# First block of a hybrid encoder step: g read from PSUM, other banks for the fourth tile, pinned casts and products, one weight's upper parts cast by GpSimd

## The chip, the core and the metric

The kernel runs on one core of one Trainium2 chip. A core has five engines that run their own instruction queues and meet at semaphores: TensorE (PE, whose weight loads are listed apart as PEld), VectorE (DVE), ScalarE (ACT), GpSimd (POOL) and SyncE (SP, which here only issues transfers). The metric is the device time of one launch in microseconds (us); lower is better. The median of three runs is given.

## The reference

One layer over 2048 prompt frames and 32 sample frames of width 1024 (2080 rows in all):

```python
def layer(h, p, ...):
    hn = rmsnorm(h, g_mix)
    proj = hn @ w_in                       # 1024 x 3072
    hA, bA, cA, zA, vB, zB = split(proj)   # six pieces of width 512
    yA = bA * conv3(cA * hA) * silu(zA)
    yB = pooled(vB) @ pool_w * pool_scale * silu(zB)
    h = h + concat(yA, yB) @ w_out
    gate = sigmoid(rmsnorm(h, g_ple) @ w_ple_gate)
    return h + (p @ w_ple) * gate
```

A last RMSNorm closes it; the last rows of `cA * hA` and `vB` are returned as states. `rmsnorm` multiplies each row by one over the root of its mean square, and each column by g. The change touches the first product alone: `hn @ w_in` for the first frames.

## The kernel before

**Precision.** Every float32 operand of a product is split in two fp32r parts (`split`, L77): `hi` is a cast, `lo` is the operand minus `hi`. A product is three: hi x hi, hi x lo, lo x hi. The cast runs on ACT (L78), the difference on DVE (L79).

**Blocks.** The rows are cut into five blocks of 416 frames (`NB`). Blocks 0 and 1 are the first group. A block comes in as four tiles of x: three of 128 rows and a short one of 32; the short tile of block 0 (`short0`, 64 rows) holds the 32 rows of block 0 and those of block 1 together. Each tile is loaded by SP (L393), its squares are summed on ACT (L89), POOL makes the root in two steps (`ms`, L70, and `rstd`, L74), DVE scales the tile by the root and by g (`normal`, L407), PE turns it in two halves of four 128-column pieces each (`turn`, L417), and the turned halves are split into the operand `B0` (`put`): "11" and "21" for block 0, "12" and "22" for block 1. From the parts of both blocks DVE makes differences (f, L659) for later products.

**g.** g_mix comes in as one row; PE spreads it over 128 partitions with a matrix of ones, in two halves of 512 columns, each into a bank of PSUM (`gm_0`, `gm_1`, L376). DVE copies both into `g_bc` in SBUF (L377), and all scaling reads `g_bc`.

**PSUM.** There are eight banks: six in the ring of `bank` and two in the ring of `tbank`. In block 0 the turned halves (`pt0_...`) take the six large ones, the fourth tile's two halves come round to the first ones again. `idle` is a small bank into which PE turns the identity, to no purpose but to be busy (`keep_busy`, L618; 30 times in all).

**The first products.** Three weights of unit 0 come first: zb, v and c (`weights`, their raw forms are `raw_first...`, whose space first serves as scrap for the squares). For each, the hi x hi part of block 0 is made first (`upper_parts`, L582, tiles `zb_first`, `v_first`, `c_first`), the parts with lo follow (`lower_parts`), then block 1 by `project` (L565, tiles `zb`, `v`, `c`). In between PE turns block 1's tiles (`pt1_...`) and the small vectors (`pv`, L694). Block 1's short part is turned first (`pt1_3_...`), since it lies in the tile that is there already; ACT also copies each turned half of block 1 back over its tile (L657), which frees the bank.

**Order.** A scheduler orders the instructions of each engine; those marked by `keep_in_program_order` stay in the order of the program. Every engine runs its queue strictly in order, so an instruction that waits holds all behind it.

Of the kernel before, what the change touches and what calls it, by code (L numbers as in the profile page):

```python
# [12 lines left out]
ALU = mybir.AluOpType  # L13
PSUM = bass.MemoryType.PSUM

P = 128
D = 1024
# [18 lines left out]
def trunk(ctx, tc, x_p, x_s, c_conv, c_pool, p_p, p_s, g_mix, w_in, conv_w, conv_b, pool_w,  # L36
# [39 lines left out]

    def split(hi, lo, src, eng=nc.vector):  # L77
        ins = nc.scalar.copy(hi, src)  # L78
        eng.tensor_tensor(lo, src, hi.bitcast(F32), op=ALU.subtract)  # L79
        return ins  # L80
# [250 lines left out]
    with ExitStack() as s1:  # L331
# [16 lines left out]

        def put(piece, src):

            return split(piece[:, :, 0], piece[:, :, 1], src)

# [18 lines left out]
        ones = ftile("ones").rearrange("p k n -> p (k n)")[:1, :P]  # L371
        nc.vector.memset(ones, 1.0)
        for half in range(2):
            cs = slice(half * NH, half * NH + NH)
            pg = tbank(f"gm_{half}")
            nc.tensor.matmul(pg, ones, gm_row[:, cs], start=True, stop=True)  # L376
            nc.vector.tensor_copy(g_bc[:, cs], pg)  # L377


# [24 lines left out]

        def normal(x, later=False, cs=slice(0, D)):
            xt, n, r = x
            ins = nc.vector.scalar_tensor_tensor(xt[:n, cs], xt[:n, cs], r[:n], g_bc[:n, cs], op0=ALU.mult,  # L407
                                                 op1=ALU.mult)
            if later:
                tc.keep_in_program_order(ins)  # L410

        def turn(x, half, name, get=tbank, later=False):
            xt, n, _ = x
            pt = get(name)
            for k in range(KH):
                kk = half * KH + k
                ins = nc.tensor.transpose(pt[:, k * P:k * P + n], xt[:n, kk * P:(kk + 1) * P], ident[:n, :n])  # L417
# [101 lines left out]

        def weights(kind, j, name):  # L520

            if first_w:
                return first_w.pop(0)
            raw = raw_weight(kind, j, name, lambda name: raw_of.pop(kind) if kind in raw_of else raw_ring(name))
            out = []
            for half in range(2):
                out.append(wtile(f"w_{name}_{half}"))
                put(out[-1], raw[:, half * KH:half * KH + KH])
            return out
# [30 lines left out]

        def half_product(ps, lhs, b, start, stop=True):

            for k in range(KH):
                for q, (x, y) in enumerate(((0, 0), (0, 1), (1, 0))):
                    nc.tensor.matmul(ps[:, :NB], lhs[:, k, x], b[:, k, y], start=start and k + q == 0,  # L565
                                     stop=stop and k == KH - 1 and q == 2, skip_group_check=True)

        begun = {}

        def project(ps, w, tb, between=None):  # L570
            x = hn[tb]
            for half in range(2):
                half_product(ps, w[half], x[half], half == 0, half == 1)
                if between and not half:
                    between()
# [9 lines left out]
        def upper_parts(kind, w, tb):  # L585

            ps = bank(f"{kind}_first")
            for half in range(2):
                part_of(ps, w, tb, half, 0, 0, start=half == 0)
            begun[kind] = ps  # L590
# [21 lines left out]
        B0.update(six(0))  # L612
        idle = tbank("idle")

        def keep_busy(n):

            for _ in range(n):
                tc.keep_in_program_order(nc.tensor.transpose(idle[:, :P], ident, ident))  # L618
# [21 lines left out]
        def second_block():  # L640
# [8 lines left out]
            for c, cs in [spans[3], *spans[:3]]:  # L649
# [60 lines left out]
        class Unit:  # L710
# [44 lines left out]
            def mix(self, b):  # L755
# [955 lines left out]
```

## Time and profile before

| | us |
|---|---|
| median of three runs (920.5 to 921.92) | 921.82 |
| the profiled execution, whole | 921.55 |
| its span, first to last instruction | 919.8 |
| PE busy in the span | 907.4 (99%) |
| DVE busy | 723.6 (79%) |
| ACT busy | 478.9 (52%) |
| POOL busy | 153.6 (17%) |

The granted TensorE clock is 0.998 of full speed over the span. Times in a trace are counted from the span's start; a row of a timeline gives start, duration, engine, line, operation, what it writes and reads, how many are merged, and in brackets the idle time before it with what ended it. A row of the chain of waits gives start, length and the work that everything later waited for. A busy time of merged rows runs from the first start to the last end; on DVE and ACT one instruction starts some 0.08 before the one ahead has ended.

### The profile page before, as it was taken

The numbers are of one execution on the slowest core, as the hardware profiler recorded it, in microseconds if no ns is written. First come the engines' busy times: TensorE is split into PE (matmuls) and PEld (weight loads), VectorE is DVE, ScalarE is ACT, GpSimd is POOL, SyncE is SP. The second block draws the span as 40 slices with busy tenths as digits, with TensorE's granted clock in tenths as the row PEclk, the third lists the DMA queues.
The fourth block names the chain that finished last, engine by engine and source line by source line (L and its number), as shares of the span: only waits on it lengthen the run. The fifth ranks groups of instructions, "written<-read, shape, count | busy, mean of one in ns | idle before, by whom it ended". The sixth has DMA issues, their size and how long they took to land.

```text
span 919.8 us, 13006 instructions
## 1 busy us (share of the span) xinstructions
PE 907.4 (99%) x4515; PEld 821.9 (89%) x4515; DVE 723.6 (79%) x1235; ACT 478.9 (52%) x883; POOL 153.6 (17%) x271
## 2 busy tenths in 40 slices
PE   8999999999999999999999999999999999999996
PEld 7999999999999999999999987888877868878885
DVE  6996989999488989785778679665554798888875
ACT  7744565554345555443545446344334875465555
POOL 4111322212001111000000011111111002323333
PEclk9999999999999999999999999999999999999999
DMA  8255595769935555457765359756775885799892
GB/s 261 79 156 151 162 274 157 210 201 314 414 114 162 181 160 187 118 178 264 203 177 170 125 192 295 254 190 184 252 216 170 307 263 146 185 222 241 205 264 101
DMA packets 140734, 186.37 MB, mean 203 GB/s; under 512 B 12060, under 2 KB 111260, under 8 KB 139389
## 3 DMA queue, kind: packets, MB, share of 16 engines
q1 hardware_dynamic: 120237, 126.33, 45.1%
q0 software_dynamic: 17696, 53.71, 20.0%
q10 hardware_dynamic: 2736, 5.51, 1.8%
q8 instruction: 35, 0.57, 0.3%
q14 instruction: 30, 0.25, 0.1%
HBM read 128.93 MB, written 56.56 MB: 202 GB/s over the span
## 4 chain that ended last, share of the span: by engine, by line
PE 89%; DVE 4%; DMA 3%; ACT 1%; issue 1%; SPq 0%; POOL 0%; DVEq 0%; ACTq 0%; POOLq 0%
PE x_o L168 9%; PE x_zbv L565 7%; PE x_ch L565 7%; PE x_zab L565 7%; PE x_g L168 6%; PE e L103 5%; PE z_o L168 4%; PE z_zbv L565 3%; PE z_ch L565 3%; PE z_zab L565 3%; PE b L565 3%; PE za L565 3%; PE h L565 3%; PE z_g L168 3%; PE v L565 2%; PE c L565 2%
## 5 line engine op out<-in xcount | busy, mean ns | idle before, releaser
L103 PE MATMUL e<-wq,pps 128*128 128x512 f32 (+1 forms) x156 | 38.9, 399 | 0.2 <-ACT pps L78 0.2
L78 ACT CAST y_S<-y_fS 128x512 fp32r<-128x512 f32 x32 | 19.3, 621 | 38.0 <-PE x_o L168 20.0
L168 PE MATMUL x_o<-wo_b,y_S 128*128 128x512 f32 x128 | 35.7, 390 | 0.0
L168 PE MATMUL x_g<-wg_b,g_S 128*128 128x512 f32 x128 | 35.7, 389 | 0.0
L565 PE MATMUL z_zbv<-B,w_zbv_S 128*128 128x416 f32 x168 | 34.2, 352 | 0.0
L565 PE MATMUL x_ch<-B,w_ch_S 128*128 128x416 f32 x168 | 34.1, 351 | 0.0
L565 PE MATMUL z_zab<-B,w_zab_S 128*128 128x416 f32 x168 | 34.1, 351 | 0.0
L565 PE MATMUL x_zab<-B,w_zab_S 128*128 128x416 f32 x168 | 34.0, 351 | 0.0
L565 PE MATMUL x_zbv<-B,w_zbv_S 128*128 128x416 f32 x168 | 34.0, 351 | 0.0
L565 PE MATMUL z_ch<-B,w_ch_S 128*128 128x416 f32 x168 | 34.0, 351 | 0.0
L1438 POOL DMA_DIRECT2D e<-h_d x28 | 24.9, 908 | 53.8 <-DVE e L1435 46.3
L103 PEld LDWEIGHTS e<-wq,pps 128*128 128x128 f32 (+1 forms) x156 | 27.4, 182 | 6.9 <-ACT pps L78 0.5
L70 POOL TENSOR_SCALAR ms_x<-ssq_x 128x1 f32<-128x1 f32 (+2 forms) x18 | 12.3, 682 | 122.7 <-ACT junk L89 118.5
L565 PEld LDWEIGHTS x_zab<-B,w_zab_S 128*128 128x128 f32 x168 | 31.3, 188 | 0.4
L565 PEld LDWEIGHTS x_zbv<-B,w_zbv_S 128*128 128x128 f32 x168 | 31.4, 188 | 0.3
L565 PEld LDWEIGHTS z_ch<-B,w_ch_S 128*128 128x128 f32 x168 | 31.4, 188 | 0.3
L565 PEld LDWEIGHTS z_zab<-B,w_zab_S 128*128 128x128 f32 x168 | 31.3, 188 | 0.3
L565 PEld LDWEIGHTS x_ch<-B,w_ch_S 128*128 128x128 f32 x168 | 31.3, 188 | 0.3
L565 PEld LDWEIGHTS z_zbv<-B,w_zbv_S 128*128 128x128 f32 x168 | 31.3, 188 | 0.4
L78 ACT CAST y<-y 128x512 fp32r<-128x512 f32 x24 | 14.8, 618 | 30.8 <-PE z_o L168 12.8
L168 PEld LDWEIGHTS x_o<-wo_b,y_S 128*128 128x128 f32 x128 | 24.0, 188 | 5.1 <-ACT c_o L1241 0.3
L168 PEld LDWEIGHTS x_g<-wg_b,g_S 128*128 128x128 f32 x128 | 24.0, 188 | 4.9
(607 smaller groups left out, 2656.2 us busy)
## 6 DMA issues: line engine op xcount, KB each, us to landing
y<-y_d SPq DMA_DIRECT2D x16, 512.0 KB, 6.2
x<-in_x_prompt_dram SPq DMA_DIRECT2D x16, 512.0 KB, 5.7
h_d<-x SPq DMA_DIRECT2D x16, 512.0 KB, 2.6
hn<-h_d SPq DMA_DIRECT2D x61, 128.0 KB, 6.6
xt<-in_x_prompt_dram SPq DMA_DIRECT2D x15, 512.0 KB, 5.3
e<-e_d SPq DMA_DIRECT2D x15, 512.0 KB, 6.1
e<-h_d POOLq DMA_DIRECT2D x28, 256.0 KB, 7.0
out_dram<-e POOLq DMA_DIRECT2D x13, 512.0 KB, 4.1
```

Of the source, the lines that this page charges most:

```text
L70: nc.gpsimd.tensor_scalar(ms[:n], ssq[:n], scalar1=1.0 / D, scalar2=EPS, op0=ALU.mult, op1=ALU.add)
L78: ins = nc.scalar.copy(hi, src)
L103: nc.tensor.matmul(ps[:n], pps[:, a, k, :n], wp[k][b][:, cs], start=k + q == 0, stop=k == 1 and q == 2)
L168: nc.tensor.matmul(ps[:n], lhs[:, k, a, :n], w[b][:, k], start=start and k + q == 0, stop=k == KH - 1 and q == 2, skip_group_check=True)
L565: nc.tensor.matmul(ps[:, :NB], lhs[:, k, x], b[:, k, y], start=start and k + q == 0, stop=stop and k == KH - 1 and q == 2, skip_group_chec ...
L1438: nc.gpsimd.dma_start(ee, h_d[r:r + P, at[1] * NH:at[1] * NH + NH], accum_op=ALU.add)
```

## The change

It has six parts, all in the first block:

1. **Scaling.** Block 0's four tiles are scaled by halves (`normal_half`) that read g from its two PSUM banks. The copies into `g_bc` stay, ahead of the scaling in DVE's queue; block 1's tiles and all later scaling read `g_bc` as before.
2. **Banks.** The short tile's halves are turned into the two small banks (those of g), for block 0 and for block 1.
3. **Fillers.** `idle` goes. Fillers (17 instead of 30) are written into the bank that the next transposes or `zb_first` will overwrite.
4. **Pins.** The casts of v's and c's first weights, the products of block 1 (`project` with `tb == 1`) and the first product of `mix` stay in program order.
5. **zb's casts.** The hi parts of zb's first weight are cast by POOL (`nc.gpsimd.tensor_copy`), two casts of 128x512.
6. `split`, `put` and `weights` take the casting operation as an argument.

```diff
-    def split(hi, lo, src, eng=nc.vector):
-        ins = nc.scalar.copy(hi, src)
+    def split(hi, lo, src, eng=nc.vector, cast=nc.scalar.copy):
+        ins = cast(hi, src)
         eng.tensor_tensor(lo, src, hi.bitcast(F32), op=ALU.subtract)
         return ins
...
+        g_ps = []
         for half in range(2):
...
             nc.vector.tensor_copy(g_bc[:, cs], pg)
+            g_ps.append(pg)
...
+        def normal_half(x, half):
+            xt, n, r = x
+            cs = slice(half * NH, half * NH + NH)
+            tc.keep_in_program_order(
+                nc.vector.scalar_tensor_tensor(xt[:n, cs], xt[:n, cs], r[:n], g_ps[half][:n], op0=ALU.mult, op1=ALU.mult))
+
+        def turn(x, half, name, get=tbank, later=False, fill=0):
             xt, n, _ = x
             pt = get(name)
+            for _ in range(fill):
+                tc.keep_in_program_order(nc.tensor.transpose(pt[:, :P], ident, ident))
...
-        def weights(kind, j, name):
+        def weights(kind, j, name, cast=nc.scalar.copy):
...
-                put(out[-1], raw[:, half * KH:half * KH + KH])
+                ins = put(out[-1], raw[:, half * KH:half * KH + KH], cast)
+                if name[:5] == "first" and kind != "zb":
+                    tc.keep_in_program_order(ins)
...
-                half_product(ps, w[half], x[half], half == 0, half == 1)
+                half_product(ps, w[half], x[half], half == 0, half == 1, tb == 1)
...
             ps = bank(f"{kind}_first")
+            for _ in range(4 if kind == "zb" else 0):
+                tc.keep_in_program_order(nc.tensor.transpose(ps[:, :P], ident, ident))
...
-        keep_busy(8)
+        FILL = (6, 1), (1, 1), (4, 1), (0, 0)
         for x in (*ahead0, short0):
             for half in range(2):
-                normal(x, True, slice(half * NH, half * NH + NH))
+                normal_half(x, half)
...
-                ins = put(B0[q][:, :, :, c * P:c * P + n], turn(x, half, f"pt0_{c}_{half}", bank, True)[:, :, :n])
+                ins = put(B0[q][:, :, :, c * P:c * P + n], turn(x, half, f"pt0_{c}_{half}", bank if c < 3 else tbank, True, FILL[c][half])[:, :, :n])
                 tc.keep_in_program_order(ins)
-                keep_busy(((1, 1), (1, 12), (1, 1), (3, 2))[c][half])
...
-            made.append(weights(kind, 0, f"first{kind}"))
+            made.append(weights(kind, 0, f"first{kind}", nc.gpsimd.tensor_copy if kind == "zb" else nc.scalar.copy))
...
-                    pt = turn(x, half, f"pt1_{c}_{half}", bank, later=True)[:, :, ts]
+                    pt = turn(x, half, f"pt1_{c}_{half}", tbank if c == 3 else bank, later=True)[:, :, ts]
...
-                nc.tensor.matmul(pm[:, :NB], pw[:, 0, j], pp, start=True, stop=False)
+                ins = nc.tensor.matmul(pm[:, :NB], pw[:, 0, j], pp, start=True, stop=False)
+                if self.gi + j == 0:
+                    tc.keep_in_program_order(ins)
```

The order of the instructions changes on PE, DVE and ACT in the first 75 us, and hardly behind. PE, from the second tile's second half to the first product (a transpose reads `ident`; rows with `ident` alone are fillers; `pt0_2` is the third tile, `pt0_3` the short one). Before:

```order
L417 MATMUL pt0_1_1_239<-ident_70,xt_0_1_170 128x128 x4
L618 MATMUL idle_198<-ident_70 128x128 x12
L417 MATMUL pt0_2_0_258<-ident_70,xt_0_2_178 128x128 x4
L618 MATMUL idle_198<-ident_70 128x128
L417 MATMUL pt0_2_1_266<-ident_70,xt_0_2_178 128x128 x4
L417 MATMUL pt0_3_0_274<-ident_70,xt_0_3_186 128x64 x4
L618 MATMUL idle_198<-ident_70 128x128 x3
L417 MATMUL pt0_3_1_284<-ident_70,xt_0_3_186 128x64 x4
L618 MATMUL idle_198<-ident_70 128x128 x2
L582 MATMUL zb_first_360<-B0_0_195,w_firstzb_0_294 128x416 x4
```

Now:

```order
L426 MATMUL pt0_1_1_235<-ident_70,xt_0_1_170 128x128 x4
L423 MATMUL pt0_2_0_243<-ident_70 128x128 x4
L426 MATMUL pt0_2_0_243<-ident_70,xt_0_2_178 128x128 x4
L423 MATMUL pt0_2_1_254<-ident_70 128x128
L426 MATMUL pt0_2_1_254<-ident_70,xt_0_2_178 128x128 x4
L426 MATMUL pt0_3_0_262<-ident_70,xt_0_3_186 128x64 x4
L426 MATMUL pt0_3_1_269<-ident_70,xt_0_3_186 128x64 x4
L602 MATMUL zb_first_343<-ident_70 128x128 x4
L595 MATMUL zb_first_343<-B0_0_195,w_firstzb_0_277 128x416 x4
```

Four fillers stand ahead of the third tile where twelve did, none between the short tile's halves, and four ahead of the first product. On ACT the two casts of zb, which stood ahead of and behind the short tile's second cast, are gone; on POOL they stand behind the short tile's root and ahead of block 1's first root.

DVE, from block 1's last scaling (`xt_1_2`) to the low part of its first turned half (`pt1_3_0`); w_h is the next weight, V the values of block 0. Before:

```order
L407 SCALAR_TENSOR_TENSOR xt_1_2_318<-xt_1_2_318,rstd_x1_2_337,g_bc_84 128x1024
L79 TENSOR_TENSOR pw_343<-raw_pw_352,pw_343 128x512
L79 TENSOR_TENSOR w_h0_0_0_656<-raw_h0_0_654,w_h0_0_0_656 128x4x128
L782 TENSOR_TENSOR win1_0_0_0_0_422<-V_0_0_356 128x416
L79 TENSOR_TENSOR B0_12_320<-pt1_3_0_430,B0_12_320 128x4x32
```

Now:

```order
L409 SCALAR_TENSOR_TENSOR xt_1_2_301<-xt_1_2_301,rstd_x1_2_320,g_bc_84 128x1024
L79 TENSOR_TENSOR pw_326<-raw_pw_335,pw_326 128x512
L791 TENSOR_TENSOR win1_0_0_0_0_409<-V_0_0_339 128x416
L79 TENSOR_TENSOR B0_12_303<-pt1_3_0_417,B0_12_303 128x4x32
L800 TENSOR_TENSOR pl_0_0_0_0_411<-win1_0_0_0_0_409,cnt_110 128x1
```

The difference of w_h has moved behind (it follows block 1's low parts now).

DVE, from the pooled values' low part (pp) to the low parts of block 1's third tile (`pt1_2`), the last that block 1's products need. Before:

```order
L79 TENSOR_TENSOR pp_0_0_421<-pl_0_0_0_0_424,pp_0_0_421 128x416
L79 TENSOR_TENSOR B0_2_197<-pt1_0_1_454,B0_2_197 128x4x128
L79 TENSOR_TENSOR B0_12_320<-pt1_1_0_462,B0_12_320 128x4x128
L79 TENSOR_TENSOR B0_2_197<-pt1_1_1_470,B0_2_197 128x4x128
L695 COPY vec_342<-pv_478 128x112
L79 TENSOR_TENSOR B0_12_320<-pt1_2_0_491,B0_12_320 128x4x128
L659 TENSOR_TENSOR f0_1_0_580<-xt_1_0_307,B0_0_195 128x512
L79 TENSOR_TENSOR B0_2_197<-pt1_2_1_499,B0_2_197 128x4x128
```

Now:

```order
L79 TENSOR_TENSOR pp_0_0_408<-pl_0_0_0_0_411,pp_0_0_408 128x416
L702 COPY vec_325<-pv_465 128x112
L79 TENSOR_TENSOR B0_12_303<-pt1_1_0_449,B0_12_303 128x4x128
L666 TENSOR_TENSOR f0_1_0_567<-xt_1_0_290,B0_0_195 128x512
L79 TENSOR_TENSOR B0_2_197<-pt1_1_1_457,B0_2_197 128x4x128
L79 TENSOR_TENSOR B0_12_303<-pt1_2_0_478,B0_12_303 128x4x128
L79 TENSOR_TENSOR B0_2_197<-pt1_2_1_486,B0_2_197 128x4x128
```

One difference (f0) has moved ahead of the low part of `pt1_2_0`, and the low part of `pt1_0_1` ahead of pp.

More of the change, by code (lines that the diff above doesn't have):

```diff
@@ L347, in wtile, with put @@
             return wr.tile([P, KH, 2, P], F32R, tag="w", name=name)
-        def put(piece, src):
-            return split(piece[:, :, 0], piece[:, :, 1], src)
+        def put(piece, src, cast=nc.scalar.copy):
+            return split(piece[:, :, 0], piece[:, :, 1], src, cast=cast)
         def ftile(name):
@@ L403, in x_tile, with normal @@
             return x_stat(x_load(name, rows), squares=squares)
-        def normal(x, later=False, cs=slice(0, D)):
+        def normal(x, later=False):
             xt, n, r = x
-            ins = nc.vector.scalar_tensor_tensor(xt[:n, cs], xt[:n, cs], r[:n], g_bc[:n, cs], op0=ALU.mult,
-                                                 op1=ALU.mult)
+            ins = nc.vector.scalar_tensor_tensor(xt[:n], xt[:n], r[:n], g_bc[:n], op0=ALU.mult, op1=ALU.mult)
             if later:
                 tc.keep_in_program_order(ins)
-        def turn(x, half, name, get=tbank, later=False):
+        def normal_half(x, half):
[4 more added lines that the diff above has]
+        def turn(x, half, name, get=tbank, later=False, fill=0):
             xt, n, _ = x
             pt = get(name)
+            for _ in range(fill):
+                tc.keep_in_program_order(nc.tensor.transpose(pt[:, :P], ident, ident))
             for k in range(KH):
@@ L559, in pair_weights, with half_product @@
             return make
-        def half_product(ps, lhs, b, start, stop=True):
+        def half_product(ps, lhs, b, start, stop=True, later=False):
             for k in range(KH):
                 for q, (x, y) in enumerate(((0, 0), (0, 1), (1, 0))):
-                    nc.tensor.matmul(ps[:, :NB], lhs[:, k, x], b[:, k, y], start=start and k + q == 0,
-                                     stop=stop and k == KH - 1 and q == 2, skip_group_check=True)
+                    ins = nc.tensor.matmul(ps[:, :NB], lhs[:, k, x], b[:, k, y], start=start and k + q == 0,
+                                           stop=stop and k == KH - 1 and q == 2, skip_group_check=True)
+                    if later:
+                        tc.keep_in_program_order(ins)
         begun = {}
@@ L612, in trunk @@
         B0.update(six(0))
[L613 to L618, printed above, removed]
-        keep_busy(8)
+        FILL = (6, 1), (1, 1), (4, 1), (0, 0)
         for x in (*ahead0, short0):
             for half in range(2):
-                normal(x, True, slice(half * NH, half * NH + NH))
+                normal_half(x, half)
         for c, x in enumerate([*ahead0, short0]):
@@ L759, in mix @@
                 pm = tbank(f"pm_{self.tag}_{b}")
-                nc.tensor.matmul(pm[:, :NB], pw[:, 0, j], pp, start=True, stop=False)
+                ins = nc.tensor.matmul(pm[:, :NB], pw[:, 0, j], pp, start=True, stop=False)
+                if self.gi + j == 0:
+                    tc.keep_in_program_order(ins)
                 nc.tensor.matmul(pm[:, :NB], pw[:, 0, j], pq, start=False, stop=False)
```

## The prediction

> **What bounds the kernel now.** I read the table by stretch first, to see where PE is short of work, then the chain of waits for the first 60 us, then the timelines of VectorE (DVE), GpSimd (POOL), ScalarE (ACT) and TensorE (PE, its weight loads PEld) there, since the diff touches only the first block.
>
> ```profile
> 0.00:40.00 40.00, 36.39 (x202) 32.44 (x203) 31.21 (x55) 29.48 (x58) 13.20 (x51) 1.00 0.62 186
> 40.00:919.80 879.80, 871.04 (x4314) 789.47 (x4313) 692.38 (x1181) 449.40 (x825) 140.38 (x220) 1.00 0.68 203
> ```
>
> Columns: length, then busy time and count of PE, PEld, DVE, ACT, POOL, then clock and DMA. PE is the bound: it lacks 3.6 us in the first 40 us, and 8.8 us in the 880 that follow, none of which the diff touches. So whatever brings the first block's products forward without holding PE later comes off the end one for one. The chain of waits shows who holds PE before them:
>
> ```profile
> 8.91 1.15 ACT junk L89 x2
> 10.58 0.76 POOL ms_x L70
> 11.41 0.95 POOL rstd_x L74
> 12.39 1.41 DVE xt L407 x2
> ...
> 26.80 0.51 ACT V L832
> ...
> 28.01 0.60 DVE w_h L79
> ...
> 29.34 0.28 ACT xt L657
> 29.66 0.66 PE pt L417 x4
> ```
>
> Two places: the scaling of the fourth tile of x (12.39), and a copy of a turned tile (29.34) that frees the bank PE wants at 29.66. Between them PE runs without a gap.
>
> **Scaling from PSUM.** The chain alternates between POOL's root and DVE's scaling, so I looked at how long POOL's two tiny steps take beside what DVE does (timelines; start, duration):
>
> ```profile
> 6.83 1.40 DVE L407 SCALAR_TENSOR_TENSOR xt<-xt,rstd_x,g_bc 128x512 f32<-128x512 f32 x2
> 7.07 0.55 POOL L70 TENSOR_SCALAR ms_x<-ssq_x 128x1 f32<-128x1 f32 x1 [0.46 <-ACT raw_firstv L89]
> 7.70 0.94 POOL L74 TENSOR_TENSOR rstd_x<-ms_x,nhalf 128x1 f32<-128x1 f32 x1
> 8.68 1.41 DVE L407 SCALAR_TENSOR_TENSOR xt<-xt,rstd_x,g_bc 128x512 f32<-128x512 f32 x2 [0.45 <-POOL rstd_x L74]
> 8.85 0.63 POOL L70 TENSOR_SCALAR ms_x<-ssq_x 128x1 f32<-128x1 f32 x1 [0.21 <-ACT raw_firstc L89]
> 10.53 1.42 DVE L407 SCALAR_TENSOR_TENSOR xt<-xt,rstd_x,g_bc 128x512 f32<-128x512 f32 x2 [0.44 <-POOL rstd_x L74]
> 11.41 0.94 POOL L74 TENSOR_TENSOR rstd_x<-ms_x,nhalf 64x1 f32<-64x1 f32 x1
> 19.82 1.62 POOL L70 TENSOR_SCALAR ms_x<-ssq_x 128x1 f32<-128x1 f32 x1 [7.47 <-ACT junk L89]
> 788.11 0.19 POOL L70 TENSOR_SCALAR ms_f<-ssq_f 128x1 f32<-128x1 f32 x1 [2.38 <-ACT junk L89]
> 788.39 0.56 POOL L74 TENSOR_TENSOR rstd_f<-ms_f,nhalf 128x1 f32<-128x1 f32 x1
> 788.14 0.69 DVE L1432 TENSOR_TENSOR c_g<-x_g,c_g 128x512 f32<-128x512 f32 x1 [2.58 <-PE x_g L168]
> ```
>
> At 788 DVE reads one operand from PSUM (x_g), and POOL beside it takes 0.19 and 0.56. In the first block DVE reads xt and g_bc, both in SBUF, and the same steps take 0.55 to 0.63 and 0.94: they end when DVE's operation ends (6.83+1.40 = 8.23, and the root of 7.70 ends at 8.64; 19.82+1.62 = 21.44, just where DVE's run of weight differences ends, row at 20.11 below). So POOL is held while DVE has two SBUF operands, not when one is in PSUM. Reading g from its banks frees it. A pair of halves occupies DVE 13.72-12.39 = 1.33 (next fence but one); I take the same with g in PSUM. The two copies into g_bc stay ahead in DVE's queue, so the first pair stays at 6.83. The second: root ready at 7.07+0.19+0.08+0.56 = 7.90, DVE free at 8.16, so 8.16 for 8.68. The third: 8.85+0.83 = 9.68, plus 0.03 to DVE: 9.71 for 10.53. The fourth: its squares are summed by 10.06 (the chain's 8.91+1.15), root at 10.14+0.83 = 10.97, DVE free at 9.71+1.33 = 11.04: **11.04 for 12.39, a gain of 1.35**. If PSUM cost DVE 0.07 per half, the fourth pair is 0.15 later; nothing suggests less than zero.
>
> **Fillers and banks on PE.**
>
> ```profile
> 9.79 0.87 PEld L417 LDWEIGHTS pt<-ident,xt 128*128 128x128 f32 x4
> 10.86 0.57 PEld L417 LDWEIGHTS pt<-ident,xt 128*128 128x128 f32 x4
> 11.40 1.34 PEld L618 LDWEIGHTS idle<-ident 128*128 128x128 f32 x12
> 12.71 0.47 PEld L417 LDWEIGHTS pt<-ident,xt 128*128 128x128 f32 x4
> 14.45 0.32 PEld L417 LDWEIGHTS pt<-ident,xt 64*128 64x128 f32 x4 [0.61 <-DVE B L79]
> 15.88 1.45 PEld L582 LDWEIGHTS zb_first<-B,w_firstzb 128*128 128x128 f32 x8
> ```
>
> A transpose takes 0.213 until about 11.1 (the four of 9.79 and a filler reach 10.86, 1.07 for five) and 0.11 after (twelve fillers, 1.34). Twelve fillers held the third tile until 12.71 though it was scaled at 11.2; the fourth waited for its bank (0.61) until DVE had made the first low part. Now: six fillers, first transpose when the first half is scaled (7.6), four groups and three fillers at 0.213 to 10.8, the fourth group at 11.35, four fillers 11.8, third tile to 12.8, the fourth (scaled by 12.4, its banks are g's, already read) to 13.4, four fillers to 13.85.
>
> **Casts.**
>
> ```profile
> 9.97 2.33 ACT L78 CAST B<-pt 128x512 fp32r<-128x512 f32 x4
> 15.11 0.62 ACT L78 CAST w_firstzb<-raw_firstzb 128x512 fp32r<-128x512 f32 x1
> 898.85 2.20 POOL L1574 TENSOR_TENSOR hg<-h,g_bc 128x512 f32<-128x512 f32 x1 [4.75 <-DVE h L1503]
> 898.69 1.22 DVE L79 TENSOR_TENSOR wl<-wlr,wl 128x1024 fp32r<-128x1024 f32 x1
> xt<-in_x_prompt_dram SPq DMA_DIRECT2D x6, 512.0 KB, 6.3
> 5.71 0.40 SPq L515 DMA_DIRECT2D raw_firstzb<-in_w_in_dram  x1
> ```
>
> ACT's last two x casts follow the fourth tile to 13.9, and no weight cast of zb stands between them any more (about 2 x 0.6 off ACT). POOL's cast is not in the trace. Nearest row: a two-operand 128x512 multiply, 2.20, of which DVE's two-SBUF operation held it until 899.91, so 1.14 of its own. With one operand it should not exceed that; below, ACT's 0.62. I take 1.14: the raw weight is issued at 5.71 and lands 6.3 later, 12.0 (by then POOL is done with roots), so 13.15 and 14.3. DVE meanwhile works on one PSUM operand at a time (scaling, then low parts), so by the row at 788 it does not hold POOL. The Trainium skill, GPSIMD Engine Reference, section 4.1 (Engine selection), tells one to keep elementwise work on VectorE, and its section 3.1 gives 769 ns for 512 elements of a lean loop; an estimate from that page is 13.55 for both casts, and the sum stays as it is. So zb_first starts at 13.9 for 15.88 (**1.95 earlier**), its second half at 14.7 finds its weight. At 2.20 a cast it would wait until 16.4, 0.25 earlier than now (15.88+4x0.19 = 16.64). Behind the casts in POOL's queue stand the second block's roots, which nobody can ask for before ACT has summed those tiles (18.6 now), so POOL is free again 4 us before. ACT, without zb's casts, reaches w_firstv at 13.9 and w_firstc at 15.0; the latter's load, issued at 8.90 on the same queue, may hold it to 15.2, and PE asks for it at 13.9+3.0 = 16.9: covered by 1.1. If that cover went (a load later than 16.3), c_first would wait by as much, and so would all of PE behind it.
>
> **Where the gain is cut.** PE then runs to the second block's transposes 1.95 earlier. DVE does not: it is busy without a gap from the low parts on, and so is 1.35 earlier at every step.
>
> ```profile
> 13.72 4.06 DVE L79 TENSOR_TENSOR B<-pt,B 128x512 fp32r<-128x512 f32 x8
> 20.11 1.28 DVE L79 TENSOR_TENSOR w_firstc<-raw_firstc,w_firstc 128x512 fp32r<-128x512 f32 x2
> 26.12 1.29 DVE L407 SCALAR_TENSOR_TENSOR xt<-xt,rstd_x,g_bc 128x1024 f32<-128x1024 f32 x1 [0.72 <-POOL rstd_x L74]
> 30.05 0.14 PEld L694 LDWEIGHTS pv<-ident,rows 112*128 112x128 f32 x1
> 33.15 0.68 DVE L79 TENSOR_TENSOR B<-pt,B 128x512 fp32r<-128x512 f32 x1
> 33.98 2.08 PEld L565 LDWEIGHTS zb<-B,w_firstzb 128*128 128x128 f32 x11
> 57.77 1.89 PEld L565 LDWEIGHTS za<-B,w_za 128*128 128x128 f32 x10
> ```
>
> The second block's scaling still reads g_bc and still alternates with POOL (2.0 a tile), only 1.35 earlier: its last tile 24.77. The fourth tile's second half is now turned into the two small banks, so the six large ones no longer hold up the transpose of 29.66; the vectors' transpose (pv) takes one of the small banks and waits for the same copy instead, with c_first's second part queued behind it on PE. DVE's w_h difference (0.60) no longer stands before that copy, so the copy ends at 29.62-1.35-0.60 = 27.67 and PE passes pv 2.35 earlier than its 30.05. But the first product of the second block (zb, 33.98) needs at its second load, 34.17, the low part that DVE ends at 33.83. In the new order w_h (0.60) goes out from ahead of this and one difference f (0.60) comes in: it ends at 32.48. PE would ask at 34.17-2.35 = 31.82, waits 0.7, and goes on at 32.52: **1.65 earlier**. Behind it PE and DVE keep step: DVE's w_za difference moves behind others and by the same cadence of 0.60 ends near 56.7, just where PE's third load of za asks (57.77+2x0.19-1.65 = 56.5; up to 0.2 lost, which I leave to the range). The rest shifts as a whole.
>
> The sum: -1.35 (scaling) -0.30 (the slack of 34.17 over 33.83, less a signal) = -1.65 on the profiled execution's 921.55, so 919.9; that execution lies 0.27 under the median of 921.82, from which it would be 920.17. I predict **920.1**.
>
> **Rivals.**
> *PE sets the pace (0.25).* If DVE has a gap, say w_firstc's cast waits for its load, POOL's first root slips in and the second block is scaled 0.7 earlier. Then the whole 2.35 counts: 921.55-2.35, 919.2. Against it: the 1.62 at 19.82 shows no such gap now.
> *The clock switches later (0.10).* Fewer fillers keep PE busy; at 0.213 all the way (0.16 for the short ones, twice the 0.08 of row 14.45) zb_first starts at 16.6, and after the bank's stall is gone some 0.3 remain: 921.2. The rows before 11.1 are full in both orders, which speaks against it. The Trainium skill, TensorE: Matmul & The Clock Gate, Part 1, has a free-running window of about 3.4 us of sustained work before full rate; the trace agrees with some window (slow to 11.1), and by that page the switch could fall at 14.5 as well.
> *POOL is starved (0.08), slower.* If DVE's low parts hold POOL although one operand is in PSUM, the casts get in only when DVE stops for want of w_firstzb, at 12.37+4.0 = 16.4. With 2.20 each they end at 20.8, and zb_first's second half is 4.2 later than 16.64. Of that 1.0 comes back, since PE no longer stops before 29.66 (it is through with its 20 transposes at 26.7+8x0.08+12x0.11 = 28.6): 921.55+3.2, 924.7. With 1.14 each they end at 18.7, 2.0 late, and 1.0 remains: 922.6. So it decides from casts that end after 17.6. The rows at 788 speak against it, the length of POOL's steps beside two SBUF operands for it.
>
> **How the numbers follow.** 0.2% is 1.84 us, about what a measurement here can tell from none. The forecast (0.57; its own range 919.4 to 920.8) straddles that line: 0.28 faster, 0.29 same. PE's pace adds 0.23 faster, 0.02 same; the clock 0.10 same; starvation 0.06 slower, 0.02 same. With 0.01 moved to slower for what no case names: faster 0.51, same 0.42, slower 0.07. The range runs from a little under PE's pace, 918.8, to no gain, 921.7.
>
> **What would show it.** Right: first-block roots at 0.56, the fourth scaling pair near 11.0, POOL's casts under 1.2 each and done by 14.3, zb_first's first load near 13.9, and a PE wait of some 0.7 for DVE's low part at the second block's zb, near 31.8. Wrong: roots still at 0.94, halves that take longer than 0.75, zb_first waiting for POOL, or no wait at 31.8 (then it is PE's pace).

## The result

The changed kernel took 920.63 us, median of 22 executions (919.39 to 923.07), the kernel before 922.11 (22 executions, 920.5 to 924.28). The ratio is 0.9984, with a 95% interval of 0.9978 to 0.999: faster by about 1.5 us. The forecast was 920.1, its range 918.8 to 921.7. The chances were laid at a line of 0.2%: the middle of the result falls short of it, on the side that had 0.42, and the interval holds the line.

The number came out near the forecast, but the experiments show that it is a sum of other parts: the scaling gave less than was counted for it, and something that the prediction had not priced, a drop of TensorE's clock in about a third of the executions of the kernel before, is gone. That the two nearly cancel in the total is luck.

### The profile page after: what moved, and what is told of

Its sections match the earlier page's. It is cut to its first block, busy times and chain, and to the rows that moved or that the text cites. A ratio compares the mean times of both kernels' runs of the same rounds, so it can differ in the third digit from the quotient of the medians.

```text
span 918.2 us, 12979 instructions
## 1 busy us (share of the span) xinstructions
PE 906.3 (99%) x4503; PEld 820.7 (89%) x4503; DVE 723.1 (79%) x1235; ACT 476.8 (52%) x881; POOL 154.1 (17%) x273
## 4 chain that ended last, share of the span: by engine, by line
PE 94%; DVE 1%; DMA 1%; POOL 1%; issue 1%; ACT 1%; SPq 0%; ACTq 0%; DVEq 0%; POOLq 0%
PE x_o L168 9%; PE x_g L168 9%; PE x_zbv L576 7%; PE x_ch L576 7%; PE x_zab L576 7%; PE e L103 5%; PE z_g L168 5%; PE z_o L168 4%; PE z_zbv L576 3%; PE z_ch L576 3%; PE z_zab L576 3%; PE za L576 3%; PE b L576 3%; PE h L576 3%; PE zb L576 2%; PE v L576 2%
## 5 line engine op out<-in xcount | busy, mean ns | idle before, releaser
L1245 DVE TENSOR_TENSOR c_o<-x_o,x 128x512 f32<-128x512 f32 x14 | 9.7, 691 | 23.8 <-PE x_o L168 23.8
```

The source lines that it names most:

```text
L1245: add = lambda o, a, b: nc.vector.tensor_tensor(o, a, b, op=ALU.add)
```

## The profile after

The table by stretch of the changed kernel (length; busy time and count of PE, PEld, DVE, ACT, POOL; granted clock; share of the DMA engines; GB/s):

```profile
0.00:40.00 40.00, 36.31 (x194) 31.83 (x195) 31.55 (x56) 27.61 (x56) 12.27 (x53) 1.00 0.63 186
40.00:918.20 878.20, 869.97 (x4311) 788.82 (x4309) 691.52 (x1180) 449.17 (x825) 141.79 (x220) 1.00 0.67 204
```

PE is busy for as long as before in the first 40 us (36.31 for 36.39), and what follows lacks 8.23 instead of 8.76. The span is 918.2 for 919.8. Read as a pair, these two profiles mislead twice. The first block as a whole moved by little. These are rows of the changed kernel's timelines there (start, duration, and so on as before):

```profile
8.91 1.06 ACT L89 ACTIVATE raw_firstc<-xt 128x1024 bf16<-128x1024 f32 x1 [2.03 <-DMA xt<-in_x_prompt_dram]
6.85 2.71 DVE L417 SCALAR_TENSOR_TENSOR xt<-xt,rstd_x,gm 128x512 f32<-128x512 f32 x4
11.01 2.78 DVE L417 SCALAR_TENSOR_TENSOR xt<-xt,rstd_x,gm 128x512 f32<-128x512 f32 x4 [1.44 <-POOL rstd_x L74]
11.81 0.54 POOL L74 TENSOR_TENSOR rstd_x<-ms_x,nhalf 64x1 f32<-64x1 f32 x1
12.32 1.17 POOL L78 CAST w_firstzb<-raw_firstzb 128x512 fp32r<-128x512 f32 x2
13.71 2.47 DVE L79 TENSOR_TENSOR B<-pt,B 128x512 fp32r<-128x512 f32 x4
14.83 1.44 PEld L595 LDWEIGHTS zb_first<-B,w_firstzb 128*128 128x128 f32 x8
32.66 0.19 PEld L576 LDWEIGHTS zb<-B,w_firstzb 128*128 128x128 f32 x1
33.59 2.56 PEld L576 LDWEIGHTS zb<-B,w_firstzb 128*128 128x128 f32 x14 [0.74 <-DVE B L79]
57.75 2.38 PEld L576 LDWEIGHTS za<-B,w_za 128*128 128x128 f32 x13 [0.25 <-DVE w_za L79]
```

POOL's root takes 0.54 beside DVE's scaling (0.94 before). Yet the low parts start at 13.71, as before (13.72), because the third x tile's load landed late: ScalarE could start its squares only at 8.91, in the first profile of the kernel before at 7.62. The last four rows show where it ends: PE starts zb_first at 14.83 (15.88 before), reaches the second block's zb at 32.66, waits 0.74 for DVE's low part, and makes the second load at 33.59 (34.17 before), only 0.58 earlier; at za's third load it waits again, 0.25, and is 0.40 earlier there (57.75 for 57.77+2x0.19 = 58.15).

The other 1.2 us of this pair's difference arise behind that, where the change leaves the kernel as it is, most of it near the end: PE starts z_g at 759.93, for 760.67 before, which is still only 0.74 earlier. The chain of waits of the kernel before held three loads there, and that of the changed kernel none:

```profile
778.63 8.21 DMA e<-h_d
802.88 5.74 DMA hn<-h_d
857.50 8.35 DMA hn<-h_d
```

In the further profiles such loads come and go in either kernel. So a pair of profiles can't say where 1.5 us went; several profiles of each, and timed executions, have to.

## The experiments

**The changed kernel and the kernel before, profiled again.**

> The changed kernel once more, unaltered, as the yardstick for the runs beside it. Ratio to the kernel before 0.9978 to 0.999, so 1 to 2 us less. In its profile GpSimd's roots take 0.55 each in the first block, the second block's scaling ends 1.35 earlier than before if the x loads land as before (7.57 for the third tile, 9.5 for the fourth), and TensorE waits some 0.7 for VectorE's low part at the second load of zb in the second block. If loads land later, as in the first profile of it (third tile 8.88), the scaling ends at the same time as before and that gain is missing from the execution: then the load, not the instruction, sets it.

> The kernel before once more, for a second profile of it. Theory (the load of the first block's third x tile lands at different times from execution to execution, 7.6 to 9.1 so far): with a timely load zb's second load in the second block stands near 34.2, as in its first profile; with a load that lands 1.3 late, near 35 to 35.5. If the time of landing belonged to the kernel rather than to the execution, it would land near 7.6 again.

> The kernel before, a third profile. Reading to test: from the start of the third x tile's squares on ScalarE to the start of VectorE's low parts it takes 6.0 to 6.1 (7.62 to 13.72 and 8.63 to 14.62 so far), and from there to the second load of zb in the second block 20.45. If the landing of the third tile's load belongs to the execution, the squares start anywhere from 7.6 to 9.1.

> The kernel before, a fourth profile, for the same reading: 6.0 to 6.1 from the third tile's squares to the low parts, 20.45 from there to the second load of the second block's zb.

The changed kernel again: 920.61 us, ratio 0.9985 (0.9976 to 0.9994). The kernel before: single times of 921.27, 924.22 and 923.58, each with its profile. From the rows of all these profiles, in us, with those of two experiments below that leave the scaling as it is in the change:

| profile | third tile's squares start | low parts start | between | zb's second load | from the low parts |
|---|---|---|---|---|---|
| before, first | 7.62 | 13.72 | 6.10 | 34.17 | 20.45 |
| before, second | 8.63 | 14.62 | 5.99 | 35.08 | 20.46 |
| before, third | 8.99 | 14.54 | 5.55 | 36.14 | 21.60 |
| before, fourth | 8.45 | 14.15 | 5.70 | 35.76 | 21.61 |
| changed, first | 8.91 | 13.71 | 4.80 | 33.59 | 19.88 |
| changed, again | 9.15 | 13.88 | 4.73 | 34.02 | 20.14 |
| e3 (more fillers) | 8.24 | 13.38 | 5.14 | 33.53 | 20.15 |
| e6 (squares apart) | 8.27 | 13.30 | 5.03 | 33.44 | 20.14 |

First, the landing belongs to the execution: in the kernel before alone the squares start anywhere from 7.62 to 8.99. Second, counted from there, the change brings the low parts forward by 0.91 (mean 5.84 to 4.93), not by 1.35. The other profiles that read g from PSUM in the first block (e2, e4, e5, e9, e11) lie at 4.73 to 5.16 and leave that mean as it is (4.91 over all nine). My expected 6.0 to 6.1 for every profile of the kernel before was wrong: VectorE can have run out of scaling when the load lands, and then nothing holds POOL. In the third profile the third and fourth roots take 0.55 and 0.54:

```profile
7.87 0.94 POOL L74 TENSOR_TENSOR rstd_x<-ms_x,nhalf 128x1 f32<-128x1 f32 x1
10.51 0.55 POOL L74 TENSOR_TENSOR rstd_x<-ms_x,nhalf 128x1 f32<-128x1 f32 x1
12.63 0.54 POOL L74 TENSOR_TENSOR rstd_x<-ms_x,nhalf 64x1 f32<-64x1 f32 x1
```

A late load alone doesn't do it: in the second profile the squares start at 8.63, yet these two roots take 0.94 and 0.93; VectorE's scaling began late there as well (8.27, in the first profile 6.83).

Third, from the low parts on, 20.45 became 20.14 where DVE sets the pace. (In the changed kernel's first profile it is 19.88, since POOL's first root of the second block happened to be through 0.27 sooner.) But in two profiles of the kernel before it is 21.6. There PE was late, and this is why. PE in the first profile of the kernel before:

```profile
11.07 0.60 PE L417 MATMUL pt<-ident,xt 128*128 128x128 f32 x4
14.45 0.46 PE L417 MATMUL pt<-ident,xt 64*128 64x64 f32 x4 [0.38 <-DVE B L79]
15.91 1.77 PE L582 MATMUL zb_first<-B,w_firstzb 128*128 128x416 f32 x8
19.02 1.67 PE L582 MATMUL c_first<-B,w_firstc 128*128 128x416 f32 x8
```

and in its third profile, with the row of the windows over 16 to 20 us (the clock is the third number from the end):

```profile
9.76 0.60 PE L417 MATMUL pt<-ident,xt 128*128 128x128 f32 x4
15.27 0.46 PE L417 MATMUL pt<-ident,xt 64*128 64x64 f32 x4 [1.90 <-DVE B L79]
16.98 3.02 PE L582 MATMUL zb_first<-B,w_firstzb 128*128 128x416 f32 x8
21.35 1.67 PE L582 MATMUL c_first<-B,w_firstc 128*128 128x416 f32 x8
```
```profile
16.00:20.00 4.00, 4.00 (x17) 3.64 (x16) 4.00 (x9) 3.81 (x9) 0.00 (x0) 0.57 0.65 236
```

In the first, four transposes take 0.60 from 11.07 on (1.06 until then): PE came to full speed late, so it reached the short tile late and waited only 0.38 for its bank. In the third it was at full speed by 9.76, was through with the full tiles sooner, and then waited 1.90 for the bank that DVE's first low part frees. After that wait the granted clock over 16 to 20 us is 0.57, the eight zb_first products take 3.02 for 1.77, and from zb_first's start to c_first's start 4.37 pass for 3.11: 1.26 lost. The fourth profile shows the same after a wait of 1.23, with 4.67 for 3.11. In the changed kernel the short tile's halves go to the small banks, the wait for a bank is gone, and the clock stays:

```profile
16.00:20.00 4.00, 4.00 (x23) 3.98 (x22) 4.00 (x9) 3.18 (x6) 0.93 (x1) 1.00 0.56 188
```

Over the whole span such a drop shows as a clock of 0.995 or 0.996 for 0.997 to 0.999, and each timed execution has its clock on record. The four profiles match: 0.998 and 0.997 without the drop, 0.995 and 0.996 with it. Of the executions timed beside the experiments, and all 33 of the changed kernel:

| kernel | executions | mean us | clock 0.996 or less | the others, mean |
|---|---|---|---|---|
| before (three chips) | 83 | 922.17 | 29, mean 923.16 | 921.63 |
| changed (two sets) | 33 | 920.65 | none | 920.65 |

So the mean gain of 1.52 splits: 921.63-920.65 = 0.98 in executions without a drop, and 29/83 x (923.16-921.63) = 0.53 from the drops that are gone. The split is rough, because the share of drops differs by chip: 7 of 33 executions on the one chip where the changed kernel was timed beside them (the chip of its other set is not on record), 22 of 50 on the other two. On that one chip alone the gain of 1.46 splits into 1.20 and 0.26. On the other two chips the experiments that keep the change's scaling and small banks for the first block's short tile (e3, e5, e6; 34 executions) have no clock under 0.997 either. That the low clocks of the timed executions all come from this place is inferred from the two profiles that show it.

**The scaling reads SBUF again.**

```diff
-  nc.vector.scalar_tensor_tensor(xt[:n, cs], xt[:n, cs], r[:n], g_ps[half][:n], ...)
+  nc.vector.scalar_tensor_tensor(xt[:n, cs], xt[:n, cs], r[:n], g_bc[:n, cs], ...)
```

> The change with the first block's scaling reading g from SBUF again, all else left. Theory (the sum): the scaling from PSUM frees GpSimd's roots and carries 1.35 of the gain; without it the roots are near 0.94 again beside the scaling and the time is 1.2 to 1.4 above the changed kernel, ratio to the kernel before about 0.9997. Rival (the order, the banks and the casts carry it): roots slow again but the time stays within 0.3 of the changed kernel, ratio about 0.9984.

Measured: 921.84 us, ratio 1.0005 (0.9995 to 1.0014): the whole gain is gone, and the rival with it. By the medians the loss is 1.23 (920.61 for the changed kernel beside it), as expected. But it is not the loss of the scaling alone. Two of 11 executions again have a clock of 0.996, although the short tile still has the small banks, and the profile shows what else is in it:

```profile
11.84 0.94 POOL L74 TENSOR_TENSOR rstd_x<-ms_x,nhalf 64x1 f32<-64x1 f32 x1
12.74 1.68 POOL L78 CAST w_firstzb<-raw_firstzb 128x512 fp32r<-128x512 f32 x2
12.81 2.15 DVE L417 SCALAR_TENSOR_TENSOR xt<-xt,rstd_x,g_bc 64x512 f32<-64x512 f32 x2 [0.44 <-POOL rstd_x L74]
14.00 0.46 PE L426 MATMUL pt<-ident,xt 64*128 64x64 f32 x4 [0.78 <-DVE xt L417]
15.01 0.46 PE L426 MATMUL pt<-ident,xt 64*128 64x64 f32 x4 [0.56 <-DVE xt L417]
```

With both operands in SBUF, the fourth tile's two halves take 2.15 beside POOL's casts, in the change 1.40 (0.736 each), and the casts 1.68 for 1.17. So it costs both engines, and e1 undoes more than the freed roots: with the scaling in SBUF, POOL's casts do harm. The Trainium skill, SBUF — State Buffer, section "SBUF: two separate sides", describes an exclusive lock that a VectorE operation with two SBUF inputs and a GpSimd operation that reads SBUF take in turn, in either direction; both directions are seen here.

PE waits again just ahead of zb_first, 0.78 and 0.56, now for the scaled halves. This profile has no drop of the clock; that the two low clocks come from these waits is not shown.

**Zb's casts back on ScalarE.**

```diff
-  weights(kind, 0, f"first{kind}", nc.gpsimd.tensor_copy if kind == "zb" else nc.scalar.copy)
+  weights(kind, 0, f"first{kind}", nc.scalar.copy)
```

> The change with zb's first weight cast by ScalarE again, all else left. It puts two casts of about 0.6 in front of ScalarE's later casts, so zb_first starts 1.0 to 1.3 later on TensorE. Theory (VectorE's low part sets the second block): TensorE's wait at the second block's zb, 0.74 in the changed kernel, swallows most of it: time 0.2 to 0.5 above the changed kernel. Rival (TensorE sets the pace): all of it counts, 1.0 to 1.3 above.

Measured: 920.48 us, ratio 0.9987 (0.9978 to 0.9995), as the changed kernel beside it (920.61). ScalarE, too, has its casts done almost in time, since it makes them ahead of w_firstv's:

```profile
13.99 1.16 ACT L78 CAST w_firstzb<-raw_firstzb 128x512 fp32r<-128x512 f32 x2
14.68 1.43 PEld L595 LDWEIGHTS zb_first<-B,w_firstzb 128*128 128x128 f32 x8 [0.37 <-ACT w_firstzb L78]
27.09 0.68 DVE L79 TENSOR_TENSOR w_h<-raw_h,w_h 128x512 fp32r<-128x512 f32 x1
33.63 0.68 DVE L666 TENSOR_TENSOR f<-xt,B 128x512 f32<-128x512 f32 x1
32.72 4.59 PEld L576 LDWEIGHTS zb<-B,w_firstzb 128*128 128x128 f32 x24
```

zb_first waits 0.37 for them, not the 1.0 to 1.3 that I expected, and the time does not show it. But the edit moved more than the casts: the scheduler also put w_h's difference ahead of block 1's low parts again and the first f behind them, and PE has no wait left at the second block's zb (32.72). So as a whole this kernel is as fast with ScalarE's casts; what the casts alone are worth isn't separated from DVE's new order.

**More fillers.**

```diff
-  FILL = (6, 1), (1, 1), (4, 1), (0, 0)
+  FILL = (6, 1), (1, 1), (12, 1), (0, 0)
```

> The change with eight more filler transposes on TensorE ahead of the third tile's first half (12 in place of 4; they compute nothing that is used). At 0.11 each (warm) they take 0.88 of TensorE's time before zb_first. Theory (VectorE's low part sets the second block, TensorE waits 0.74 there): time within 0.3 of the changed kernel, and TensorE's wait at the second block's zb shrinks by what zb_first starts later. Rival (TensorE sets the pace): 0.9 above the changed kernel.

Measured: 920.8 us, ratio 0.999 (0.9981 to 0.9999), beside 920.74 for e6 on the same chip. Eight fillers more don't cost their 0.88, but they don't test the rival either, since they don't hold up zb_first. It starts 1.14 behind the low parts (13.38), in the changed kernel 1.12 (14.83-13.71):

```profile
13.49 0.57 PEld L426 LDWEIGHTS pt<-ident,xt 64*128 64x128 f32 x8 [0.17 <-DVE xt L417]
14.52 1.44 PEld L595 LDWEIGHTS zb_first<-B,w_firstzb 128*128 128x128 f32 x8
```

The fillers fill time in which PE would have waited for the scaled short tile, as it still does, 0.17 (without them, in e6, 0.52 and 0.33). What speaks against PE's pace is the wait for DVE's low part at the second load of zb: 0.75 here, 0.74 in both profiles of the changed kernel. (By its FILL and the four ahead of zb_first the changed kernel has 18 fillers, not the 17 named above.)

**Squares apart.**

```diff
-  ahead0 = [x_tile(f"0_{c}", [x_rows(0, c)], in_raw(kind)) for ...]
+  ahead0 = [x_tile(f"0_{c}", [x_rows(0, c)], in_raw(kind) if c < 2 else junk) for ...]
```

> The change with the third tile's squares written to the common scrap buffer, not into the buffer that c's first weight is loaded to, so this load needn't wait for the third tile's load and squares. Theory (the load is covered): c's weight lands 1 to 2 earlier, ScalarE's cast of it no longer waits 1.1, the second block's squares start up to 1.1 earlier, but GpSimd's roots there wait for VectorE in any case: within 0.3 of the changed kernel. Rival (the late load is what keeps the gain of the scaling from showing): 0.5 to 1.1 under the changed kernel.

Measured: 920.74 us, ratio 0.9984 (0.9975 to 0.9992), no gain. My expectation that the weight would land 1 to 2 earlier was wrong: ScalarE still waits 0.91 for it. SyncE's queue says why (the column after the start is the time that the issue takes):

```profile
7.67 1.76 SPq L395 DMA_DIRECT2D xt<-in_x_prompt_dram  x1
9.47 0.43 SPq L524 DMA_DIRECT2D raw_firstc<-in_w_in_dram  x1
```

The weight's load stands right behind the issue of an x load that takes 1.76, so here the squares aren't what holds it; in the changed kernel's first profile SyncE waits 0.2 for them.

**The fourth tile's second half in large banks.**

```diff
-  pt = turn(x, half, f"pt1_{c}_{half}", tbank if c == 3 else bank, later=True)[:, :, ts]
+  pt = turn(x, half, f"pt1_{c}_{half}", bank, later=True)[:, :, ts]
```

> The change with the fourth tile's second half turned into the six large banks again, as before. Theory (VectorE's and ScalarE's chain, not the banks, sets the second block): TensorE waits for a large bank ahead of the third tile's turn, but no more than it now waits for ScalarE's copy ahead of the vectors' transpose: time within 0.3 of the changed kernel. Rival (the bank stall is what the change removes): 0.5 to 1.0 above it, and e1's loss would then be shared with the scaling.

Measured: 921.27 us, ratio 0.9992 (0.998 to 1.0004). The interval overlaps the changed kernel's and reaches no change, so up to some 0.6 may be lost. The profile doesn't show a loss: from the low parts (12.81) to zb's second load (32.67) it is 19.86, as in the changed kernel's first profile. PE does wait 1.01 for a bank in between, and the wait for DVE's low part at zb's second load shrinks to 0.32. This part stays open.

**One difference of the first Strassen column behind.** The low parts of the second block's third tile go ahead of one f and of h's low part on DVE, by an order that is written in:

```diff
-  op(t1, p12, part("11", 0))
+  behind(op(t1, p12, part("11", 0)), (2, 1))
...
+  if kind == "h":
+      behind(lows[0], (2, 1))
```

> The change with one difference f of the first Strassen column (0.60 on VectorE) and h's low part put behind the low parts of the second block's third tile. Theory (VectorE's low part sets it): the low part ends 0.60 earlier, TensorE's wait at the second load of zb shrinks from 0.74 to 0.1 to 0.2, and the time falls by 0.4 to 0.6 under the changed kernel (ratio to before about 0.9979). Rival (something else is late next, as the differences are now later for ScalarE and h's weights): the wait shrinks, but the time is the same or higher.

Measured: 920.03 us, ratio 0.9983 (0.9974 to 0.9991), with 920.61 for the changed kernel beside it: in the expected direction, but the intervals overlap. PE's wait shrank from 0.74 to 0.48, not to 0.1 or 0.2, and the waits show who is late next:

```profile
31.44 1.29 DVE L87 TENSOR_TENSOR B<-pt,B 128x512 fp32r<-128x512 f32 x2 [0.24 <-ACT B L86]
33.40 0.69 DVE L87 TENSOR_TENSOR B<-pt,B 128x512 fp32r<-128x512 f32 x1 [0.67 <-ACT B L86]
32.78 3.32 PEld L586 LDWEIGHTS zb<-B,w_firstzb 128*128 128x128 f32 x18 [0.48 <-DVE B L87]
```

DVE now waits for ScalarE's casts, which alternate with its copies of the turned tiles.

**Both blocks' scaling from PSUM.**

```diff
             for x, _ in xs:
-                normal(x, True)
+                for half in range(2):
+                    normal_half(x, half)
...
-  turn(x, half, f"pt0_{c}_{half}", bank if c < 3 else tbank, True, FILL[c][half])
+  turn(x, half, f"pt0_{c}_{half}", bank, True, FILL[c][half])
```

> The change with the second block's scaling, too, by halves from g's banks (six halves of about 0.74 in place of three of 1.28), so that g's banks are kept to 26 us and the short tile is turned into the large banks again. Theory (the scaling's two SBUF operands hold GpSimd's root back, and VectorE's chain sets the end): GpSimd's roots run beside the scaling, which takes about 4.5 in place of 5.3 and 0.72 idle before each of the last two is gone: the low parts of the second block start 0.9 to 1.5 earlier; the short tile's turn waits for a large bank, which puts zb_first 0.3 to 0.6 later, covered by TensorE's wait of 0.74. Time 0.6 to 1.2 under the changed kernel. Rival (TensorE's pace, or ScalarE's casts and copies, is late next): within 0.3 of the changed kernel.

Measured: 919.58 us, ratio 0.9978 (0.9969 to 0.9987). Its 11 executions have a mean of 919.85, those of e6 and e3 on the same chip 920.72 and 921.04. It is the fastest of the study. Rows of its timelines:

```profile
14.03 1.06 PE L426 MATMUL pt<-ident,xt 64*128 64x64 f32 x8 [1.10 <-DVE B L79]
15.62 1.44 PEld L595 LDWEIGHTS zb_first<-B,w_firstzb 128*128 128x128 f32 x8
21.70 4.04 DVE L417 SCALAR_TENSOR_TENSOR xt<-xt,rstd_x,gm 128x512 f32<-128x512 f32 x6 [0.72 <-POOL rstd_x L74]
22.93 0.55 POOL L74 TENSOR_TENSOR rstd_x<-ms_x,nhalf 128x1 f32<-128x1 f32 x1
32.69 1.32 PEld L576 LDWEIGHTS zb<-B,w_firstzb 128*128 128x128 f32 x7
```

The six halves run in one piece, 4.04, where the three whole tiles with their waits for POOL took from 21.83 to 27.12 in the change. The short tile waits 1.10 for its large bank, so zb_first starts later (15.62 for 14.83), but PE has no wait left at the second block's zb (the row at 32.69 has none in brackets): now PE sets the pace. Part of this can be DVE's order, which the scheduler put back to that of the kernel before (w_h's difference ahead of the low parts, the first f between the third tile's two). None of its 11 executions has a clock under 0.997, though the wait is back; on the same chip 13 of 27 of the kernel before have one.

**The short tile in one large bank.** The same kernel, but both halves of the short tile share one bank:

```diff
+  t3 = bank("pt0_3")
...
-  turn(x, half, f"pt0_{c}_{half}", bank, ...)
+  turn(x, half, ..., lambda _: t3[:, half * KH * w:(half + 1) * KH * w], ...)
```

> The kernel that scales both blocks from g's banks, with both halves of the short tile turned into one large bank in place of two, so that zb_first waits for one release less on VectorE's low parts. Theory: zb_first starts 0.5 to 0.8 earlier than 15.62; ScalarE's cast of the third tile's first half (31.37 to 32.0 there) and VectorE's low part behind it are late next, so TensorE waits 0.4 to 0.7 at the second block's zb again and the time falls by 0 to 0.3. Rival (TensorE's pace alone set that kernel): 0.5 to 0.8 less.

Measured: 924.12 us, ratio 1.0017 (1.0008 to 1.0026): slower, against both theories. PE in its profile:

```profile
13.85 0.46 PE L426 MATMUL pt<-ident,xt 64*128 64x64 f32 x4 [0.44 <-DVE B L79]
17.04 0.46 PE L426 MATMUL pt<-ident,xt 64*128 64x64 f32 x4 [2.72 <-DVE B L79]
17.84 2.48 PE L595 MATMUL zb_first<-B,w_firstzb 128*128 128x416 f32 x8
20.11 2.53 PE L595 MATMUL v_first<-B,w_firstv 128*128 128x416 f32 x8
```
```profile
20.00:22.00 2.00, 2.00 (x7) 1.90 (x7) 0.99 (x3) 1.97 (x4) 0.74 (x2) 0.50 0.96 271
```

The second half waits until DVE has read the first half out of the shared bank, and DVE has six other low parts ahead of that: 2.72. The clock then falls to half, and the first two groups of eight products take 2.48 and 2.53 for 1.75 and 1.67 in the change. Seven of its 12 executions have a clock of 0.996 or less. It lost what it should have won, but it shows a wait and then a half clock a third time, brought on by the edit itself. What the drop costs can't be read off here: its seven executions with a low clock have a mean of 923.96, the other five 924.16.

## Why the prediction was right, and where it wasn't

**GpSimd is freed: right.** The roots take 0.54 to 0.56 in the first block. PSUM as an operand costs VectorE nothing: the halves take 0.742 and 0.736 on average for 0.746 and 0.742 before. e1 shows that the gain hangs on it.

**"11.04 for 12.39, a gain of 1.35": the right mechanism, the size too large.** The step that failed is the base it was taken from. My count for the change holds: from the third tile's squares to the low parts it gives 13.72-1.35-7.62 = 4.75, and the profiles show 4.73 to 5.16. But the 6.10 before is the longest of four. It needs VectorE to be busy scaling when POOL asks; in two of the four profiles one or two of the last two roots run free. The term is 0.91 on average: 1.12 against the two profiles without a drop of the clock (6.10 and 5.99), 0.70 against the two with it. One reading under it was loose: the root of 7.70 does not end with DVE's operation (8.23) but 0.41 behind it; what the rows show is 0.94 beside two SBUF operands and 0.56 without them.

**"-0.30 (the slack of 34.17 over 33.83)": right,** 20.45 to 20.14, with DVE's low part setting the second block and a wait of 0.74 on PE for the forecast 0.7. The "up to 0.2" left to the range at za's third load was real and belonged into the sum: PE waits 0.25 there, and from zb's second load to it pass 24.16 (57.75-33.59) for 23.98 (58.15-34.17), so the gain shrinks by 0.18. With the scaling term of the profiles without a drop the terms are -1.12-0.31+0.18 = -1.25. The executions without a drop show -0.98 over all chips and -1.20 on the one chip where both kernels were timed. Four profiles of each kind can't settle it closer.

**What was missed: -0.53 from TensorE's clock (-0.26 on the one chip).** The row was quoted: the short tile "waited for its bank (0.61)". It was priced as waiting time alone, and as time that PE did not lack; "between them PE runs without a gap" passes over it. That a longer wait at this place, in executions whose clock rises early, can be followed by a half clock at zb_first and v_first, as in the two profiles, was in no term and in no rival; the rival on the clock had it switching later in the changed kernel, and neither profile of that kernel shows a drop. That the drops are gone was the second thing that the change did for the time. Which part of it keeps the clock up isn't separated: e1 has the small banks and two low clocks, e9 the large banks, a wait of 1.10 and none. By e1 the small banks alone are not enough, if its low clocks come from this place; by e9 the scaling from PSUM may be enough, as the wait there stays shorter than the 1.90 and 1.23 of the profiles with a drop.

**The casts: mis-sized without effect.** GpSimd's take 0.608 each, not 1.14, and in e2, with its other order on DVE, ScalarE does as well. The load of w_firstc did come after 16.3 (ScalarE's cast of it started at 16.79), and c_first started at 17.78, 2.95 behind zb_first, with no wait.

**The rivals.** Against PE setting the pace speaks the wait of 0.74 for DVE's low part in both profiles of the changed kernel; it came true in the profiles of e9, where DVE's second scaling was shortened, and of e2, where the first f went behind. Starved casts did not occur with PSUM operands; e1 shows them, at 0.86 each, where both operands are in SBUF.

## What to carry to other kernels

A wait on TensorE just ahead of a run of products has two prices: its own length, and a clock at half that may follow it. Look for the second in the clock of each execution, not in one profile, which may have been lucky. And before a stall between two engines is priced at its length in a profile, ask what has to be early for it to appear at all: here the stall of GpSimd's root by VectorE's two SBUF operands vanished in part by itself in two of four profiles, and so the cure was worth two thirds of what the first one promised.

## What the runs showed of the hardware

- The clock can fall after a short gap. Waits of 1.90 and 1.23, each followed by a few small transposes with gaps between, were followed by a clock of half speed for 3.4 us (0.57 over 4 us is 4 x 0.43/0.5); so was one of 2.72 (e11, 0.50 over 20 to 22 us); one of 1.10 (e9) was not, nor one of 0.38. What else decides it is not shown. The Trainium skill, TensorE: Matmul & The Clock Gate, "HAM oscillation", warns of idle gaps over about 3.4 us; these were well under that, and the measurement decides.
- A drop in such a stretch costs 1.26 and 1.56 in the two profiles (4.37 and 4.67 for 3.11 from zb_first to c_first), and 1.53 on average between the executions of the kernel before with a clock of 0.996 or less and the others.
- The landing of one load, issued at the same place of the same program, varied by 1.4 us over four executions of the kernel before (squares from 7.62 to 8.99).
